# Dilated attention of a two-block network: projecting groups 1 and 2 from contiguous token tiles instead of strided ones

## The chip, the cores and the metric

The kernel runs on one core of one Trainium2 chip. The metric is device time in microseconds, from the start of the program to its end; the number given is the median of three runs.

## What is computed

Two transformer blocks over 512 latent tokens of width 1024 run one after the other. The change lies in the first mixer of the second block, a dilated attention with 15 heads of 64, in three groups of five heads. Group 0 attends to near neighbours; group 1 attends within the tokens of equal remainder modulo 4, group 2 within those of equal remainder modulo 16. What the reference does, cut to that mixer:

```python
DIL_PAIRS = ((128, 1), (512, 4), (2048, 16))

def _by_stride(t, dil):
    B, G, S, dh = t.shape
    return t.reshape(B, G, S // dil, dil, dh).transpose(0, 1, 3, 2, 4).reshape(B * G * dil, S // dil, dh)

def dilated_window_mixer(h, w_qkv, w_o, cos, sin):
    qkv = (h @ w_qkv).reshape(B, S, 3, A_HEADS, HEAD_DIM_2).transpose(2, 0, 3, 1, 4)
    q = apply_rope_2(qkv[0], cos, sin)
    k = apply_rope_2(qkv[1], cos, sin)
    v = qkv[2]
    for g, (window, dil) in enumerate(DIL_PAIRS):
        sl = slice(g * G, (g + 1) * G)
        half = window // (2 * dil)
        o, lse = banded_attention(_by_stride(q[:, sl], dil), _by_stride(k[:, sl], dil),
                                  _by_stride(v[:, sl], dil), half)
        ...
    alpha = jax.nn.softmax(jnp.stack(lses, axis=0), axis=0)
    o = jnp.concatenate([outs[g] * alpha[g][..., None] for g in range(3)], axis=1)
    return o.transpose(0, 2, 1, 3).reshape(B, S, A_HEADS * HEAD_DIM_2) @ w_o
```

## The kernel before

Activations lie feature-major in SBUF: chunk c of `X` is 128 features by 512 tokens, kept as two float32r parts, high and low, whose sum is the float32 value (class `Feat`). A product needs three matmuls per chunk, high by high, high by low and low by high (`mm`, L153 to L155). A weight unit is loaded by SyncE's queue into a `raw` buffer, of which there are three, cast by ScalarE (L135) and completed by a subtraction on VectorE (L136) into one of six `w` buffers.

`tm_gemm` (L234) makes token-major products: for each tile of 128 tokens, 8 chunks by 3 matmuls, the stationary operand being 128 tokens of `X` and the moving one 320 columns of weights here. A tile's second step, `late`, comes after the next tile's matmuls.

`mixer_a` (L1178) calls `project(g)` (L1196) for groups 1, 2, 0. Each project makes q, k and v: three products of four token tiles. A q or k tile is evicted from PSUM with a scale (L1205), rotated by four VectorE operations (L1173 to L1176), turned by three TensorE transposes (L1211) and copied into place (L1212). A v tile is copied out of PSUM into `V` (L1219). `scores` (L1223) multiplies q and k of a tile and adds the mask (L1246, L1248), takes the maximum (L1253) and the exponential (L1255). `values` (L1259) turns the probabilities (L1266) and multiplies them with `V` (L1274). Groups 1 and 2 write their output rows to DRAM (L1278), and group 0 reads them back (L1229) and merges all three.

In groups 1 and 2 the tokens of one tile are those of equal remainder modulo 4. `toks` (L1191) makes that order where the tile enters the product, by a view of `X` that takes every fourth token:

```python
return lambda a: a.rearrange("p (i r) -> p r i", r=4)[:, t, :]
```

So q, k and v come out in the order that the attention needs, and the rotation table `k_rope_a` holds one order for each group.

The program's order is set in three ways. `project(1)` is emitted alone, then `project(2)` in turns with `attention(1)`, then `project(0)` in turns with `attention(2)`, and `attention(0)` with filler from the next layer's `ple_proj`. A list scheduler that works from a timeline of its own then fixes the order on every engine. Buffers of a tag go round: three PSUM buffers `mm`, four SBUF buffers `t2`.

Of the kernel before, what the change touches and what calls it, by code (L numbers as in the profile page):

```python
# [10 lines left out]
F32 = mybir.dt.float32  # L11
# [6 lines left out]
P = 128  # L18
# [3 lines left out]
LAT = 512  # L22
# [18 lines left out]
class Feat:  # L41
    """Feature-major activations as two float32r parts: chunk c is [128 features, T tokens]."""
# [34 lines left out]
class Net:  # L77
# [54 lines left out]
    # ---------------------------------------------------------------- basics  # L132
    def split(self, hi, lo, src, eng=None):
        """hi + lo = src with two float32r parts; src in PSUM or SBUF."""
        self.nc.scalar.copy(hi, src)  # L135
        (eng or self.nc.vector).tensor_sub(lo, src, hi.bitcast(F32))  # L136
# [13 lines left out]
    def mm(self, out, l, r, first, last):  # L150
        """out += l.T @ r with l, r = (hi, lo) pairs."""
        mm = self.nc.tensor.matmul
        mm(out, lhsT=l[0], rhs=r[0], start=first, stop=False)  # L153
        mm(out, lhsT=l[0], rhs=r[1], start=False, stop=False)  # L154
        return mm(out, lhsT=l[1], rhs=r[0], start=False, stop=last)  # L155

    def mm_late(self, out, pairs, first, last):
        """The sum over (l, r) pairs of mm, the products with the low parts of r at the end."""
# [4 lines left out]
    def bias_rows(self, rows, mul=1.0):  # L163
        """Up to three rows of 512 as pairs of float32r parts: row q on partitions 32 q, 32 q + 1, zeros below."""
# [18 lines left out]
    def fm_gemm(self, X, W, cols, cb, lead=0):  # L183
        """Feature-major products: for each tuple of 128-wide column starts, out[128 cols, T] each -> cb(i, *ps).
        The first `lead` tuples run in two halves of the tokens, the first halves first."""
# [48 lines left out]
    def tm_gemm(self, X, W, c0, n, cb, br=None, k0=0, nk=None, kw0=None, toks=None, steps=False,  # L234
                slack=1, feats=None):
        """Token-major products: out[128 tokens, n cols] for each token tile -> cb(t, ps)."""
# [25 lines left out]
    def tm_pair(self, X, W, cb, kw0):  # L262
        """Token-major products with both 512-wide column halves of W, all of a token tile's in a row -> cb(t, n, ps)."""
# [31 lines left out]
    def fill_behind(self, n):  # L295
        """Filler that may not start before the tensor engine's last marked instruction."""
        with self.tc.issue_after(self.pe_mark.ins):
            self.fill(n)
# [4 lines left out]
    def transpose_in(self, src, X, t):  # L303
        """src [128 tokens, 128*nch] float32 -> token tile t of X."""
# [18 lines left out]
    def moments(self, out, halves):  # L323
        """Mean and variance of the row made of the two 512-wide pieces -> out [128, 2]."""
# [5 lines left out]
    # ---------------------------------------------------------------- per-layer vectors as columns  # L330
# [45 lines left out]
    # ---------------------------------------------------------------- ada  # L376
# [21 lines left out]
    def ada_first(self, S, x):  # L398
        """Shift and scale of the first layer's mixer, both streams: the context's on all partitions (returned as
        1 + scale, shift), the other's rows to DRAM."""  # L400
# [39 lines left out]
    def ada_out(self, l, n, o, src, nrow):  # L440
        """Modulation rows n (512 wide) of nrow streams: (src + bias), scaled for its kind -> DRAM."""
# [5 lines left out]
    def ada(self, l, n0, n1):  # L447
        """Both streams' modulation rows on the tensor engine."""
# [23 lines left out]
    def ada_vec(self, l, n0, n1):  # L472
        """The same with the sums over a partition's rows on the vector engine; the context has two rows only."""
# [38 lines left out]
    # ---------------------------------------------------------------- layer norms and modulation  # L512
    def mod_rows(self, l, s, i):
        """(1 + scale, shift) rows of modulation i (0: mixer, 1: ffn)."""
# [13 lines left out]
    def first_h(self, S, x, l, bc=None, then=None, xs=None):  # L528
        """Modulated input h of the first layer: X (Feat)."""
# [24 lines left out]
    def ln_prep(self, g, b, mod, gate):  # L554
        """Broadcast rows for a layer norm: gate, g, b and (if modulated) A, B."""
# [21 lines left out]
    def ln_finish(self, S, y, t, st_in, bc, xout, h_out, done=None):  # L577
        """y [128, 1024] token-major -> x (to DRAM xout, or kept in rms_x) and modulated h via h_out(t, h)."""
# [33 lines left out]
    # ---------------------------------------------------------------- first block: attention  # L612
    def head_norm(self, ps, nh, gain, rope_t):
        """RMS norm of nh heads of 128, gain, rotary -> SBUF tile [128, nh*128]."""
# [29 lines left out]
    def heads_T(self, src, nh, dst):  # L644
        """src [128 tok, nh*128] -> transposed heads, split into dst(hl) [128, nh, 128]."""
# [17 lines left out]
    def kv(self, l, kT, tiles):  # L663
        """For each (X, t, o, V, rotate): token tile t of X, keys (heads normed, rotated) into kT[kv][128, hl, o : o + 128],
        values into V[128, hl, tile, 256]."""
# [25 lines left out]
    def attend(self, nt, q, kT, vs, nkeys, o_dram, sums, gap):  # L691
        """One kv head: q(t) [128 d, hl, 4 heads, 128]; unnormalised O^T of heads h, h + 1 to o_dram(t, h)
        [128 d, 2, 128], the rows' sums to sums(t, h) [128, 1]."""
# [3 lines left out]
        def turned(Ps, k0):  # L697
            """Key chunks k0, k0 + 1 of two heads' probabilities, transposed."""
# [53 lines left out]
    def inverse_rows(self, sums, nt):  # L752
        """sums [128 tokens, nt, 8 heads] -> 1 / sums as rows [8 heads, tokens] in DRAM."""
# [11 lines left out]
    # ---------------------------------------------------------------- first block: merge of the branches  # L765
    def conv_gemm(self, l, S, X, convh, chains, chains2):
        """Gated input of the depthwise convolution; its taps go to `chains` (vector engine) and
        `chains2` (products on the scalar engine, sums on GpSimd)."""
# [75 lines left out]
    def pool_branch(self, l, S, X, m, between):  # L844
        """Pooling branch with its gate, added to m; `between` supplies other work."""
# [67 lines left out]
    def conv_ln(self, l, S, convh, C):  # L913
        """Layer norm and silu of the convolution, split into C."""
# [45 lines left out]
    def chunked(self, T, tag="s8"):  # L960
        """8 feature-major float32 chunks [128, T]."""
# [23 lines left out]
    def out_ln(self, S, M, W, bias, bc, xin, xout, h_out):  # L985
        """y = ALPHA x + gate (M @ W + bias); layer norm."""
# [19 lines left out]
    # ---------------------------------------------------------------- first block: ffn  # L1006
# [74 lines left out]
    # ---------------------------------------------------------------- second block  # L1081
    def rms_norm(self, xt, g):
        """x / rms(x) * g, in a new tile."""
# [10 lines left out]
    def add_out(self, X, W, x, done, k0=0, nk=None, kw0=None):  # L1094
        """x += X.T @ W, token tile by token tile; done(t, x(t)) after the second half."""
# [27 lines left out]
    def ple_proj(self, i, tag="w"):  # L1123
        """p @ w_ple_proj, halved, to DRAM."""
# [38 lines left out]
    def rope_small(self, v, r, cos, sin):  # L1163
        """In place rotation of the first 2r entries of the last dim of v [128, h, d]; cos, sin [128, 2r]."""
# [13 lines left out]
    def mixer_a(self, x, X, done):  # L1178
        nc, A = self.nc, self.A
        W = A["a_w_qkv_2"][0]  # L1180
        rp = self.sb([P, 3, 4, 32], F32, "rpa")
        nc.sync.dma_start(rp, A["k_rope_a"].rearrange("g (t p) d -> p g t d", p=P))
# [4 lines left out]
        # rows of groups 1, 2: unnormalised output, negative maxima, sums  # L1187
# [3 lines left out]
        def toks(g, t):  # L1191
            if g == 0:
                return lambda a: a[:, t * P : t * P + P]
            return lambda a: a.rearrange("p (i r) -> p r i", r=4)[:, t, :]

        def project(g):  # L1196
            tk = [toks(g, t) for t in range(4)]
            T = []
            for which in range(2):
                dst = self.sb([P, 3, 512], F32, "s8")  # L1200

                def cb(t, ps, which=which, dst=dst):
# [3 lines left out]
                    self.rope_small(q[:, 0:320].rearrange("p (h d) -> p h d", d=64), 8, rp[:, g, t, 0:16], rp[:, g, t, 16:32])  # L1206

                    def late():
# [3 lines left out]
                        nc.scalar.copy(dst[:, :, t * P : t * P + P], tp)  # L1212
# [3 lines left out]
                yield from self.tm_gemm(X, W, 960 * which + 320 * g, 320, cb, toks=tk, steps=True)  # L1216
                T.append(dst)
            V = self.sb([P, 4, 320], F32, "s8")
            yield from self.tm_gemm(X, W, 1920 + 320 * g, 320, lambda t, ps: nc.scalar.copy(V[:, t, :], ps) and None,  # L1219
# [324 lines left out]
def first_block(net, stop=None):  # L1544
# [18 lines left out]
    def mix(l, S, X, kT, vs, nkeys, rope, bc_mod, xin, xout, h_out, before_out=None, extra=None):  # L1563
# [30 lines left out]
        n = 0  # L1594
# [252 lines left out]
```

## Time and profile before

| | us |
|---|---|
| three runs | 4112.67, 4114.3, 4116.21 |
| median | 4114.3 |
| span of the profiled execution, first to last instruction | 4108.2 |
| median less span (launch and end; the profiled execution has no other time of its own listed) | 6.1 |
| TensorE busy in the span | 3835.9 (93%) |
| VectorE, ScalarE, GpSimd busy | 2729.5, 1537.3, 1055.7 |

TensorE is shown as two rows: PE, the matmuls, and PEld, the loads of stationary operands, which overlap the matmuls. The duration of a matmul overlaps its neighbours', so a stretch is best read by the distance from start to start. The granted clock (PEclk) is a share of 2.4 GHz: 1.00 is that level, 0.50 is 1.2 GHz.

### The profile page before, as it was taken

The numbers are of one execution on the slowest core, as the hardware profiler recorded it, in microseconds if no ns is written. First come the engines' busy times: TensorE is split into PE (matmuls) and PEld (weight loads), VectorE is DVE, ScalarE is ACT, GpSimd is POOL, SyncE is SP. The second block draws the span as 40 slices with busy tenths as digits, with TensorE's granted clock in tenths as the row PEclk, the third lists the DMA queues.
The fourth block names the chain that finished last, engine by engine and source line by source line (L and its number), as shares of the span: only waits on it lengthen the run. The fifth ranks groups of instructions, "written<-read, shape, count | busy, mean of one in ns | idle before, by whom it ended". The sixth has DMA issues, their size and how long they took to land.

```text
span 4108.2 us, 49603 instructions
## 1 busy us (share of the span) xinstructions
PE 3835.9 (93%) x18765; PEld 3179.4 (77%) x18765; DVE 2729.5 (66%) x3713; ACT 1537.3 (37%) x2685; POOL 1055.7 (26%) x1028
## 2 busy tenths in 40 slices
PE   7788999699898999999989999999999999999999
PEld 4678787477777887777767788889778888778887
DVE  4998799966989666789986645551354336764444
ACT  3535444234343332344324233332433224653333
POOL 3554422574544001422364200010000001420000
PEclk9789999899999999999999999999999999999999
DMA  6456322454566455321333423331223332123332
GB/s 204 118 141 212 94 62 85 116 151 153 179 217 190 154 162 166 112 67 54 99 96 115 128 86 116 119 98 45 88 86 99 96 96 78 24 67 108 98 98 92
DMA packets 544825, 469.04 MB, mean 114 GB/s; under 512 B 31734, under 2 KB 435806, under 8 KB 544586
## 3 DMA queue, kind: packets, MB, share of 16 engines
q1 hardware_dynamic: 544506, 465.61, 37.5%
q8 instruction: 147, 2.41, 0.2%
q14 instruction: 92, 0.75, 0.1%
q0 software_dynamic: 80, 0.26, 0.0%
HBM read 442.32 MB, written 23.49 MB: 113 GB/s over the span
## 4 chain that ended last, share of the span: by engine, by line
PE 61%; DVE 25%; DMA 4%; issue 4%; ACT 3%; POOL 2%; SPq 0%; POOLq 0%; ACTq 0%; DVEq 0%
PE mm L153 18%; PE mm L154 18%; PE mm L155 18%; DVE s L787 10%; DVE w L136 4%; DVE s L136 2%; DVE s L504 1%; DVE st L740 1%; DMA w<-in_w_ada 1%; DMA raw<-in_w_in 1%; ACT w L135 1%; PE acc L161 1%; PE b L1246 1%; PE b L310 1%; ACT s L135 1%
## 5 line engine op out<-in xcount | busy, mean ns | idle before, releaser
L153 PE MATMUL mm<-s,w 128*128 128x512 f32 (+1 forms) x3072 | 1125.8, 369 | 79.8 <-ACT pad L1019 20.5
L154 PE MATMUL mm<-s,w 128*128 128x512 f32 (+1 forms) x3072 | 1119.3, 365 | 10.6 <-DVE s L136 10.6
L155 PE MATMUL mm<-s,w 128*128 128x512 f32 (+1 forms) x3072 | 1117.8, 365 | 2.2 <-DVE w L136 2.2
L135 ACT CAST w<-raw 128x1024 fp32r<-128x1024 f32 (+4 forms) x673 | 689.5, 1030 | 843.1 <-PE mm L155 427.2
L136 DVE TENSOR_TENSOR w<-raw,w 128x1024 fp32r<-128x1024 f32 (+3 forms) x517 | 670.3, 1300 | 309.5 <-ACT w L135 304.5
L153 PE MATMUL mm<-w,s 128*128 128x512 f32 (+2 forms) x1960 | 766.5, 392 | 10.9 <-ACT s L135 5.3
L154 PE MATMUL mm<-w,s 128*128 128x512 f32 (+2 forms) x1960 | 756.8, 387 | 1.3 <-DVE w L136 1.3
L155 PE MATMUL mm<-w,s 128*128 128x512 f32 (+2 forms) x1960 | 753.8, 387 | 1.3 <-DVE s L136 1.3
L153 PEld LDWEIGHTS mm<-s,w 128*128 128x128 f32 x3072 | 599.3, 196 | 192.9 <-ACT pad L1019 22.7
L154 PEld LDWEIGHTS mm<-s,w 128*128 128x128 f32 x3072 | 601.5, 196 | 95.6 <-DVE s L136 12.5
L155 PEld LDWEIGHTS mm<-s,w 128*128 128x128 f32 x3072 | 600.5, 196 | 89.3 <-DVE w L136 2.6
L787 DVE SCALAR_TENSOR_TENSOR s<-pad,cols,s 128x512 f32<-128x512 f32 (+1 forms) x690 | 573.2, 873 | 1.1
L136 POOL TENSOR_TENSOR w<-raw,w 128x1024 fp32r<-128x1024 f32 (+1 forms) x156 | 418.5, 2685 | 475.9 <-ACT w L135 475.6
L153 PEld LDWEIGHTS mm<-w,s 128*128 128x128 f32 x1960 | 396.4, 202 | 91.3 <-issue 14.5
L155 PEld LDWEIGHTS mm<-w,s 128*128 128x128 f32 x1960 | 396.0, 202 | 67.1 <-DVE s L136 2.6
L154 PEld LDWEIGHTS mm<-w,s 128*128 128x128 f32 x1960 | 396.9, 203 | 64.0 <-DVE w L136 2.7
L320 POOL TENSOR_SCALAR st<-st 128x1 f32<-128x1 f32 (+2 forms) x91 | 33.3, 366 | 1215.4 <-ACT s L1086 902.1
L1101 DVE TENSOR_TENSOR s<-s,mm 128x512 f32<-128x512 f32 x80 | 54.7, 686 | 171.7 <-PE mm L155 171.7
L136 DVE TENSOR_TENSOR s<-b,s 128x256 fp32r<-128x256 f32 (+2 forms) x224 | 119.6, 546 | 51.1 <-ACT s L135 50.2
L135 ACT CAST s<-b 128x256 fp32r<-128x256 f32 (+2 forms) x224 | 104.2, 475 | 126.0 <-DVE s L136 76.0
L1117 DVE TENSOR_TENSOR t<-t 128x512 f32<-128x512 f32 x64 | 44.3, 693 | 153.4 <-ACT t L1116 153.4
L1017 POOL MEMSET pad<- 128x1 f32 x66 | 7.5, 116 | 469.6 <-DVE t L1024 463.0
(271 smaller groups left out, 4407.8 us busy)
## 6 DMA issues: line engine op xcount, KB each, us to landing
raw<-in_w_up SPq DMA_DIRECT2D x196, 512.0 KB
raw<-in_w_in SPq DMA_DIRECT2D x180, 512.0 KB
raw<-in_w_down SPq DMA_DIRECT2D x130, 512.0 KB
w<-in_w_ada SPq DMA_DIRECT2D x48, 512.0 KB
raw<-in_w_ada SPq DMA_DIRECT2D x32, 512.0 KB
s<-d SPq DMA_DIRECT2D x26, 512.0 KB
raw<-in_conv_pw_w SPq DMA_DIRECT2D x24, 512.0 KB
raw<-in_w_out SPq DMA_DIRECT2D x24, 512.0 KB
```

The lines of the kernel that those rows point to most:

```text
L135: self.nc.scalar.copy(hi, src)
L136: (eng or self.nc.vector).tensor_sub(lo, src, hi.bitcast(F32))
L153: mm(out, lhsT=l[0], rhs=r[0], start=first, stop=False)
L154: mm(out, lhsT=l[0], rhs=r[1], start=False, stop=False)
L155: return mm(out, lhsT=l[1], rhs=r[0], start=False, stop=last)
L161: self.nc.tensor.matmul(out, lhsT=l, rhs=r, start=first and n == 0, stop=last and n == len(terms) - 1)
L310: self.pe_mark = nc.tensor.transpose(ps[:, c, :], src[:, (c0 + c) * P : (c0 + c + 1) * P], self.ident)
L504: nc.vector.scalar_tensor_tensor(out=v, in0=w, scalar=c, in1=v, op0=ALU.mult, op1=ALU.add)
L740: self.mark = nc.vector.reduce_max(out=s[:, 0:1], in_=S[:, :nkeys], axis=AX.X, negate=True)
L787: nc.vector.scalar_tensor_tensor(out=o, in0=pad[:, k : k + T], scalar=self.col("dww", 8 * k + j), in1=o, op0=ALU.mult, op1=ALU.add)
L1101: nc.vector.tensor_add(x(t)[:, cs], x(t)[:, cs], ps)
L1117: nc.vector.tensor_mul(r, r, r)
```

## The change

Groups 1 and 2 are now projected like group 0, from tiles of 128 tokens that follow each other, with one rotation table. The order modulo 4 is made afterwards. For q and k it is made by the copy of the turned tile: it reads every fourth column of the PSUM tile and writes four runs of 32 columns. For v, whose tokens lie on partitions, it is made by a trip through DRAM: each tile is copied to a `t2` buffer and written to `vd`, and when all four are there one load brings them back with partition i holding rows 4 i to 4 i + 3.

```diff
-        rp = self.sb([P, 3, 4, 32], F32, "rpa")
-        nc.sync.dma_start(rp, A["k_rope_a"].rearrange("g (t p) d -> p g t d", p=P))
+        rp = self.sb([P, 4, 32], F32, "rpa")
+        nc.sync.dma_start(rp, A["k_rope_a"].rearrange("(t p) d -> p t d", p=P))
...
-        def toks(g, t):
-            if g == 0:
-                return lambda a: a[:, t * P : t * P + P]
-            return lambda a: a.rearrange("p (i r) -> p r i", r=4)[:, t, :]
-
         def project(g):
-            tk = [toks(g, t) for t in range(4)]
...
-                        nc.scalar.copy(dst[:, :, t * P : t * P + P], tp)
+                        if g == 0:
+                            nc.scalar.copy(dst[:, :, t * P : t * P + P], tp)
+                        else:
+                            nc.scalar.copy(dst.rearrange("p j (r i) -> p j r i", r=4)[:, :, :, 32 * t : 32 * t + 32],
+                                           tp.rearrange("p j (i r) -> p j r i", r=4))
...
-                yield from self.tm_gemm(X, W, 960 * which + 320 * g, 320, cb, toks=tk, steps=True)
+                yield from self.tm_gemm(X, W, 960 * which + 320 * g, 320, cb, steps=True)
...
-            yield from self.tm_gemm(X, W, 1920 + 320 * g, 320, lambda t, ps: nc.scalar.copy(V[:, t, :], ps) and None,
-                                    toks=tk, steps=True)
+            vd = self.dram([LAT, 320]) if g else None
+
+            def cb(t, ps):
+                if g == 0:
+                    nc.scalar.copy(V[:, t, :], ps)
+                    return
+                v = self.sb([P, 512], F32, "t2")[:, :320]
+                nc.scalar.copy(v, ps)
+                nc.sync.dma_start(vd[t * P : t * P + P, :], v)
+
+            yield from self.tm_gemm(X, W, 1920 + 320 * g, 320, cb, steps=True)
+            if g:
+                nc.sync.dma_start(V, vd.rearrange("(i r) d -> i r d", r=4))
...
-    out["k_rope_a"] = np.stack([rot(8, t.reshape(-1, d).T.reshape(-1)) for d in (1, 4, 4)])
+    out["k_rope_a"] = rot(8, t)
```

The change also moves instructions, since a tile of the product now needs only one token tile of `X`, and a tile of the attention needs all four turned tiles of q and k.

TensorE, where `project(1)` begins, before. `mm_21265` is the last product of the filler, L310 turns the last token tile into `X`, `mm_21319` and `mm_21353` are the q tiles 0 and 1.

```order
L155 MATMUL mm_21265<-s_3073_20869,s_3063_20838 128x512
L310 MATMUL b_3140_21275<-ident_66,s_3121_21172 128x128 x8
L153 MATMUL mm_21319<-w_21306,s_3103_21032 128x320
L154 MATMUL mm_21319<-w_21306,s_3103_21032 128x320
L153 MATMUL mm_21353<-w_21306,s_3103_21032 128x320
L154 MATMUL mm_21353<-w_21306,s_3103_21032 128x320
```

The same place in the changed kernel. The first ten matmuls of q tile 0 stand directly behind `mm_21265`; the rows begin with the eleventh:

```order
L154 MATMUL mm_21319<-w_21311,s_3104_21035 128x320
L155 MATMUL mm_21319<-w_21311,s_3104_21035 128x320
L153 MATMUL mm_21319<-w_21311,s_3105_21038 128x320
L310 MATMUL b_3140_21275<-ident_66,s_3121_21172 128x128 x8
L154 MATMUL mm_21319<-w_21311,s_3105_21038 128x320
L155 MATMUL mm_21319<-w_21311,s_3105_21038 128x320
L153 MATMUL mm_21319<-w_21311,s_3105_21038 128x320
```

Thirteen matmuls of q tile 0 have come ahead of the last transposes into `X`.

TensorE, the end of the k product of group 1, before. `t_3185` to `t_3195` are rotated k tiles, `b_3228` the first scores of group 1, `mm_21603` the last k tile's product.

```order
L155 MATMUL mm_21603<-w_21488,s_3106_21041 128x320
L1246 MATMUL b_3228_21858<-s_3172_21475,s_3145_21303 128x128
L1211 MATMUL mm_21628<-ident_66,t_3190_21594 128x128 x3
L1248 LDWEIGHTS identb_71
L1248 MATMUL b_3228_21858<-msk_21298,identb_71 128x128
L1246 MATMUL b_3228_21858<-s_3172_21475,s_3145_21303 128x128
```

The same place in the changed kernel, up to the first matmuls of v:

```order
L153 MATMUL mm_21603<-w_21488,s_3106_21041 128x320
L154 MATMUL mm_21603<-w_21488,s_3106_21041 128x320
L155 MATMUL mm_21603<-w_21488,s_3106_21041 128x320
L1206 MATMUL mm_21628<-ident_66,t_3190_21594 128x128 x3
L1206 MATMUL mm_21642<-ident_66,t_3195_21633 128x128 x3
L153 MATMUL mm_21664<-w_21651,s_3103_21032 128x320
L154 MATMUL mm_21664<-w_21651,s_3103_21032 128x320
L155 MATMUL mm_21664<-w_21651,s_3103_21032 128x320
```

The scores have left this place, so the last k tile's transposes stand directly behind the transposes of the tile before it, as they already did at the end of q.

SyncE's queue in the changed kernel, around the trip of v of group 1. `d_21648` is the DRAM buffer, `s_3199` is `V`, the `raw` loads ahead are the last of group 2's k, those between are of group 2's v, those behind of group 0's q.

```order
L141 DMA raw_22000<-in_a_w_qkv 128x2x320
L1226 DMA d_21648<-t_3208_21689 128x320
L1226 DMA d_21648<-t_3210_21717 128x320
L1226 DMA d_21648<-t_3212_21745 128x320
L141 DMA raw_22215<-in_a_w_qkv 128x3x320
L1226 DMA d_21648<-t_3214_21773 128x320
L141 DMA raw_22220<-in_a_w_qkv 128x3x320
L141 DMA raw_22225<-in_a_w_qkv 128x2x320
L1230 DMA s_3199_21647<-d_21648 128x1280
L141 DMA raw_22396<-in_a_w_qkv 128x3x320
```

Before, only the `raw` loads stood here; the four writes and the load of `V` are new, and so are their waits.

## Rows read from the trace of the kernel before

**Rows 1.** Engines over the span, from the page: busy us, share, instructions.
```profile
PE 3835.9 (93%) x18765; PEld 3179.4 (77%) x18765; DVE 2729.5 (66%) x3713; ACT 1537.3 (37%) x2685; POOL 1055.7 (26%) x1028
```

**Rows 2.** Busy time by stretch: groups 1 and 2, then group 0's projection.
```profile
core 0: us, PE busy (x) PEld busy (x) DVE busy (x) ACT busy (x) POOL busy (x), PEclk, DMA share, GB/s
2717.00:2880.00 163.00, 160.24 (x746) 155.40 (x747) 37.11 (x99) 42.59 (x105) 2.83 (x19) 0.98 0.17 49
2880.00:2942.00 62.00, 62.00 (x424) 57.44 (x424) 15.88 (x48) 19.57 (x66) 0.91 (x6) 1.00 0.20 60
```

**Rows 3.** Longest wait of PE from 2717 to 2942: total, times, longest us.
```profile
PE mm L1211 <- DVE t L1176: 2.5, 2, 2.0
```

**Rows 4.** Instructions by line and shape, 2717 to 2945: count, busy, mean ns.
```profile
L153 PE MATMUL mm<-w,s 128*128 128x320 f32 x288 | 108.3, 376 | 0.5 <-ACT s L135 0.5
```

**Rows 5.** Timeline, group 1, strided: first and last of 18 matmuls, a load.
```profile
2731.10 0.40 PE L153 MATMUL mm<-w,s 128*128 128x320 f32 x1
...
2735.07 0.40 PE L155 MATMUL mm<-w,s 128*128 128x320 f32 x1
...
2731.17 0.33 PEld L154 LDWEIGHTS mm<-w,s 128*128 128x128 f32 x1
```

**Rows 6.** Timeline, group 0, contiguous: first and last of 25 matmuls, a load.
```profile
2902.01 0.31 PE L153 MATMUL mm<-w,s 128*128 128x320 f32 x1
...
2905.53 0.31 PE L153 MATMUL mm<-w,s 128*128 128x320 f32 x1
...
2902.01 0.19 PEld L154 LDWEIGHTS mm<-w,s 128*128 128x128 f32 x1
```

**Rows 7.** Timeline of PE where group 1 begins; idle before in brackets.
```profile
2715.76 1.07 PE L310 MATMUL b<-ident,s 128*128 128x128 f32 x8 [0.53 <-DVE s L1088]
2717.29 0.54 PE L153 MATMUL mm<-w,s 128*128 128x320 f32 x1 [0.46 <-ACT s L135]
```

**Rows 8.** Timeline of PE and VectorE at the end of group 1's q.
```profile
2741.27 0.49 PE L1211 MATMUL mm<-ident,t 128*128 128x128 f32 x3
2743.72 0.52 PE L1211 MATMUL mm<-ident,t 128*128 128x128 f32 x3 [1.96 <-DVE t L1176]
...
2741.09 1.16 DVE L136 TENSOR_TENSOR w<-raw,w 128x960 fp32r<-128x960 f32 x1 [0.94 <-ACT w L135]
...
2742.60 0.83 DVE L136 TENSOR_TENSOR w<-raw,w 128x640 fp32r<-128x640 f32 x1
2743.34 0.23 DVE L1176 TENSOR_TENSOR t<-rp,rp 128x80 f32<-128x80 f32 x1
```

**Rows 9.** Timeline of PE at half clock after that wait, strided.
```profile
2746.32 0.47 PE L153 MATMUL mm<-w,s 128*128 128x320 f32 x1
...
2748.72 0.47 PE L153 MATMUL mm<-w,s 128*128 128x320 f32 x1
```

**Rows 10.** Busy time by stretch around the two falls of the granted clock.
```profile
2744.00:2748.00 4.00, 4.00 (x19) 4.00 (x17) 0.00 (x0) 0.48 (x1) 0.15 (x1) 0.73 0.55 192
2748.00:2752.00 4.00, 4.00 (x19) 4.00 (x17) 0.70 (x4) 0.44 (x1) 0.00 (x0) 0.84 0.00 0
...
2772.00:2776.00 4.00, 4.00 (x19) 3.29 (x19) 1.02 (x3) 2.81 (x14) 0.15 (x1) 0.65 0.37 122
```

**Rows 11.** Chain, contiguous 512-column matmuls at half clock, by start.
```profile
2955.00 0.43 PE mm L153
2955.43 0.43 PE mm L154
```

**Rows 12.** Line 1212, copies of turned tiles: ns min, median, max.
```profile
L1212 ACT COPY s<-mm x24: 473/480/512, 2729.9 to 2927.4; 128x384 f32<-128x384 f32 x24
```

**Rows 13.** Timeline, group 2's rows written, read back and first used.
```profile
2945.49 0.38 SPq L1278 DMA_DIRECT2D d<-row  x1
2949.20 2.56 SPq L1229 DMA_DIRECT2D s<-d  x4
2954.77 0.16 DVE L1286 TENSOR_TENSOR st<-s 128x5 f32<-128x5 f32 x1
```

More of the change, by code (lines that the diff above doesn't have):

```diff
@@ L1205, in cb @@
                     nc.scalar.activation(q[:, 0:320], ps, AF.Copy, scale=0.125 if which == 0 else 1.0)
-                    self.rope_small(q[:, 0:320].rearrange("p (h d) -> p h d", d=64), 8, rp[:, g, t, 0:16], rp[:, g, t, 16:32])
+                    self.rope_small(q[:, 0:320].rearrange("p (h d) -> p h d", d=64), 8, rp[:, t, 0:16], rp[:, t, 16:32])
                     def late():
```

## The prediction

> **What bounds the kernel now.** I began with the busy shares of the page: TensorE is busy 93% of the span, the next engine 66% [rows 1]. So the question is what TensorE does in the stretch that the change touches, and the second view, busy time by stretch, gives that: groups 1 and 2 with the attention of group 1 take 163 us, of which PE is busy 160 and the loads of stationary operands (PEld) 155; group 0's projection with the attention of group 2 takes 62 us, PE busy throughout [rows 2]. PE's longest wait in all of this totals 2.5 us [rows 3]. No other engine is busy for more than a third of either [rows 2]. The stretch is as long as TensorE's own instructions, so a gain can only come from making those shorter.
>
> The third view is the timeline of TensorE, read by distance from start to start. In group 1, whose stationary tokens lie four elements apart, 18 matmuls start within 3.97 us, 17 steps of 0.2335 us; a load of the stationary operand takes 0.33 us [rows 5]. In group 0, with the same shape but contiguous tokens, 25 matmuls start within 3.52 us, 24 steps of 0.1467 us; the load takes 0.19 us [rows 6]. The moving operand is the same 320 columns in both, the granted clock is 0.98 and 1.00 [rows 2]. The load is what differs, and in groups 1 and 2 it sets the pace.
>
> **The change, part by part.**
>
> (a) *Contiguous stationary tokens.* The trace holds 288 matmuls of 128x320 on each of three lines [rows 4], 864 for three groups, so 576 in groups 1 and 2. Each goes from 0.2335 to 0.1467 us: 576 x 0.0868 = **-50.0 us**, all on the path, as TensorE hardly waits there [rows 3]. This leans on rows of the same program, engine, shape and clock.
>
> (b) *The start of group 1.* Before, TensorE idled 0.53 us ahead of the last transposes into X and 0.46 us ahead of the first product [rows 7], because every strided tile needs all four token tiles. Thirteen matmuls now stand ahead of those transposes, 13 x 0.1467 = 1.9 us of work: **-1.0 us**.
>
> (c) *The ends of q and k.* At the end of q in group 1 two sets of transposes stand back to back, and the second waited 1.96 us for the rotation of the last tile; VectorE was held up by the subtractions of the next weights, 1.16 and 0.83 us, which stand ahead of the rotation's last step [rows 8]. That chain starts when the 18th of the tile's 24 matmuls lets go of the second weight unit. From there TensorE has six matmuls left, which cover 1.4 us now and 0.88 us then: the wait grows by 0.5 to 2.5 us. At the end of k the scores of group 1 lay between the two sets and hid the same chain. The scores need all four turned tiles now and have moved behind v, so the wait appears there too, at 2.5 us. Together **+3.0 us**. In group 2 other attention work stands between, as in group 0, which did not wait [rows 2].
>
> (d) *The granted clock.* After the wait at q the clock fell: 0.73 and 0.84 in two stretches of 4 us, so (0.27 + 0.16) x 4 x 2 = 3.4 us at 1.2 GHz; a second fall of some 2.8 us came among the scores [rows 10]. At that level strided matmuls stepped by 2.40 us / 9 = 0.267 us [rows 9], hardly slower than at 2.4 GHz. Contiguous ones lose more: 512 columns step by 0.43 us there [rows 11], which I scale to an estimated 0.269 us for 320. I allow one spell of 3.4 us behind each of the two waits: 13 matmuls x (0.269 - 0.147) = 1.6 us, twice 3.2 us. The old spells cost 0.4 + 0.3 us, which (a) left out. Net **+2.5 us**; were there no falls, it would be -0.7.
>
> (e) *Reading every fourth column.* The 16 copies of turned q and k tiles in groups 1 and 2 took 0.48 us each [rows 12]. The trace has no such copy with a step. From below I take the 0.48 us (a step gives no reason for a gain), from above twice that. Even 16 x 0.48 = 7.7 us more would lie on an engine with 43 us of work in 163 [rows 2]: the turned tiles are wanted a tile or more later, and the three PSUM buffers go round once in a tile and a half. I count 0, and keep 7.7 us for the range.
>
> (f) *The trip of v.* Eight copies go to another buffer, at no new cost; eight writes of 160 KB and two loads of 640 KB are new, 2.6 MB. The nearest row is the trip of group 2's output: written at 2945.49, read back by a load issued at 2949.20, first used at 2954.77, so 3.7 us to the second step and 9.3 us in all [rows 13]. Two weight loads stand between the last write and the load of V. They wait for buffers that are freed by about two casts and subtractions of 1.16 us each [rows 8], so I add 4 us: 13 us. Between the end of v's product and the first product with V the new order has 124 matmuls, 18.2 us, and two sets of scores. The cover holds, and I count 0; without it the bound is 2 x 9.3 = 18.6 us. Behind the waiting V load on SyncE's queue stand group 0's q weights, not wanted before group 2's v is done; GpSimd's clearing of the next t2 buffer would wait for a write four tiles back, 14 us against 3.7 us. One rotation table for three, and the smaller load, cost nothing that anything waits for.
>
> Sum: -50.0 - 1.0 + 3.0 + 2.5 = **-45.5 us**. The span was 4108.2 and would be 4062.7. The median of the runs stands 6.1 us above the span, outside the change: 4114.3 - 45.5 = **4068.8 us**. A cross-check: the old 163 us hold 576 x 0.2335 = 134.5 us of strided products, so 28 us of everything else, which the change only reorders.
>
> **The rivals.**
>
> *Stalls at every turn.* Matmuls that are faster by a third leave ScalarE and VectorE less cover for the next weights, and the wait of (c) with its fall of the clock could come at all six ends of q, k and v. Four more at 2.5 + 1.6 us are 16.4 us: 4085.2 us. For it: the same order of subtractions and rotation at each end [rows 8]. Against it: group 0 ran at exactly the new pace, with the same weights to prepare and an attention between, and TensorE was busy for 62.00 of 62 us [rows 2].
>
> *The trip of v shows.* If the weight loads ahead of V's load are late, TensorE stands before the first product with V. At 10 us for each group, that is 4088.8 us. Against it the 5 us and more of slack in (f).
>
> *The loads do not get shorter.* Then the distance in rows 5 would be due to something other than the step. The gain of (a) falls away and only the start (-1.0), the new wait at k (+2.0) and a small fall (+0.4) are left: 4115.7 us. For it: nothing in the rows. The Trainium skill, TensorE: Matmul & The Clock Gate, section LDWEIGHTS, says that the load's time goes by its columns alone; as all loads here have 128 columns, by that rule (a) would be nothing and the time would be this one. The trace disagrees: 0.33 against 0.19 us for the same 128 columns [rows 5, 6].
>
> *The clock stays down.* If the reordered first part, with two waits in 30 us, kept TensorE at 1.2 GHz through both groups, contiguous matmuls would step by 0.269 us against the old 0.2335: 576 x 0.0355 = +20.4 us, with (b) and (c) 4136.7 us, slower than before. It decides where more than (0.2335 - 0.1467) / (0.269 - 0.1467) = 71% of the matmuls run at the lower level. For it: the clock did fall after a 2 us wait [rows 8, 10]. Against it: it came back within 3.4 us, and stood at 1.00 through the whole of group 0 [rows 2].
>
> **How the numbers follow.** The forecast has 0.78, stalls at every turn 0.12, the trip 0.04, no shorter loads 0.04, the clock 0.02. A measurement of this kernel can tell 0.2%, 8.2 us, from no change. The first three cases are faster by more: 0.94. The fourth lies within: 0.04; the last is slower: 0.02. The range starts where (c) and (d) cost nothing, 4114.3 - 51.7 = 4062.6, less 2.6 us because the scheduler also shuffles the end of the block ahead; it ends at 4088, which holds the forecast with (e) on the path (4076.5) and the first rival (4085.2).
>
> **What would show it.** Right: in the changed profile the 128x320 matmuls of groups 1 and 2 step by 0.147 us and their loads take 0.19 us; the stretch from the first product to group 0's takes some 117 us in place of 163; two waits of PE for the last step of the rotation, near 2.5 us each; no wait of PE for V. Wrong: a step that stays above 0.2 us (the third rival), waits of PE for weights or rotation at more than two ends (the first), a wait of L1284 for a DMA (the second), a granted clock well below 1.00 through the stretch (the last).

## The result and the profile after

The changed kernel takes 4067.14 us (median of 4 runs, 4057.85 to 4070.36) against 4113.49 us (4 runs, 4109.56 to 4116.21) for the kernel before on the same chip: ratio 0.9883, 95% interval 0.9869 to 0.9897. It is faster by 46.4 us. The forecast was 4068.8 us, 45.5 us faster, with a range of 4060 to 4088.

Engines over the span, from the page of the changed kernel, beside [rows 1]:

```profile
PE 3785.9 (93%) x18765; PEld 3128.9 (77%) x18765; DVE 2729.4 (67%) x3713; ACT 1535.6 (38%) x2685; POOL 1059.9 (26%) x1028
```

PE's busy time went from 3835.9 to 3785.9 us with the same 18765 matmuls: 50.0 us less. That this is the size of term (a) to a tenth is luck: a second trace of the changed kernel has 3790.5 us, and the stretches below are the better reading. VectorE has the same work to 0.1 us.

Busy time by stretch, from the first 128x320 matmul of group 1 to the first of group 0, and from there to group 0's last (columns as in [rows 2]):

```profile
2709.88:2824.68 114.80, 109.96 (x743) 104.78 (x743) 37.17 (x100) 42.33 (x107) 2.98 (x20) 0.99 0.28 87
2824.68:2889.23 64.55, 64.55 (x434) 59.99 (x433) 17.16 (x50) 20.89 (x69) 1.06 (x7) 0.97 0.23 74
```

The kernel before, between the same two matmuls of groups 1 and 2:

```profile
2717.29:2878.68 161.39, 158.92 (x735) 154.07 (x735) 36.06 (x98) 41.30 (x102) 2.77 (x19) 0.98 0.16 47
```

From there to group 0's last it took 63.01 us, by the starts of its matmuls. So groups 1 and 2 became 46.6 us shorter and group 0 1.5 us longer. PE idled 114.80 - 109.96 = 4.84 us in the first stretch. What PE waited for, from 2690 to 2960 us (total us, times, longest):

```profile
PE mm L1206 <- DVE t L1176: 4.8, 2, 2.4
PE b L310 <- DVE w L136: 3.3, 1, 3.3
PE b L310 <- DVE s L136: 3.0, 1, 3.0
PE b L1276 <- ACT s L1265: 1.2, 1, 1.2
```

L1206 is L1211 of before [rows 3]: the two waits are the ends of q and of k in group 1, and they are the 4.84 us of idle time. The other three waits lie outside the two stretches. No wait is on L1284, the product with V.

Timeline of TensorE in the changed kernel (start, us, engine, instruction, idle time before it): the first product of group 1, beside [rows 7], then the end of its q, beside [rows 8] and, for the matmuls behind, [rows 5]:

```profile
2709.88 0.42 PE L153 MATMUL mm<-w,s 128*128 128x320 f32 x1 [0.42 <-ACT t L1142]
...
2725.60 0.49 PE L1206 MATMUL mm<-ident,t 128*128 128x128 f32 x3
2728.51 0.52 PE L1206 MATMUL mm<-ident,t 128*128 128x128 f32 x3 [2.42 <-DVE t L1176]
2728.78 0.39 PE L153 MATMUL mm<-w,s 128*128 128x320 f32 x1
2729.01 0.31 PE L154 MATMUL mm<-w,s 128*128 128x320 f32 x1
2729.16 0.31 PE L155 MATMUL mm<-w,s 128*128 128x320 f32 x1
2729.30 0.31 PE L153 MATMUL mm<-w,s 128*128 128x320 f32 x1
...
2729.89 0.19 PEld L155 LDWEIGHTS mm<-w,s 128*128 128x128 f32 x1
```

The matmuls start 0.147 us apart, where before it was 0.2335, and a load takes 0.19 us in place of 0.33. VectorE at the same place:

```profile
2725.94 1.16 DVE L136 TENSOR_TENSOR w<-raw,w 128x960 fp32r<-128x960 f32 x1 [0.16 <-ACT w L135]
...
2727.39 0.82 DVE L136 TENSOR_TENSOR w<-raw,w 128x640 fp32r<-128x640 f32 x1
2728.13 0.23 DVE L1176 TENSOR_TENSOR t<-rp,rp 128x80 f32<-128x80 f32 x1
```

The rotation's last step starts behind two subtractions, as in [rows 8], and TensorE starts 0.15 us after it ends. At the end of k the same rows come again, with 2.42 us of idle time.

### The profile page after: what moved, and what is told of

The parts are those of the page before. It is cut to its first block, busy times and chain, and to the rows that moved or that the text cites. A ratio compares the mean times of both kernels' runs of the same rounds, so it can differ in the third digit from the quotient of the medians.

```text
span 4056.1 us, 49639 instructions
## 1 busy us (share of the span) xinstructions
PE 3785.9 (93%) x18765; PEld 3128.9 (77%) x18765; DVE 2729.4 (67%) x3713; ACT 1535.6 (38%) x2685; POOL 1059.9 (26%) x1028
## 4 chain that ended last, share of the span: by engine, by line
PE 60%; DVE 26%; DMA 5%; issue 4%; ACT 3%; POOL 2%; SPq 0%; ACTq 0%; POOLq 0%; DVEq 0%
PE mm L153 18%; PE mm L154 18%; PE mm L155 18%; DVE s L787 10%; DVE w L136 4%; DVE s L136 2%; DVE s L504 1%; DVE st L740 1%; DMA w<-in_w_ada 1%; ACT w L135 1%; DMA raw<-in_w_in 1%; PE acc L161 1%; PE b L1256 1%; PE b L310 1%; DVE t L1024 1%
## 5 line engine op out<-in xcount | busy, mean ns | idle before, releaser
L153 PE MATMUL mm<-w,s 128*128 128x512 f32 (+2 forms) x1960 | 750.4, 384 | 11.9 <-ACT s L135 5.6
L153 PEld LDWEIGHTS mm<-s,w 128*128 128x128 f32 x3072 | 599.8, 196 | 188.0 <-ACT pad L1019 21.2
L154 PE MATMUL mm<-w,s 128*128 128x512 f32 (+2 forms) x1960 | 741.6, 379 | 1.3 <-DVE w L136 1.3
L155 PE MATMUL mm<-w,s 128*128 128x512 f32 (+2 forms) x1960 | 739.0, 379 | 1.3 <-DVE s L136 1.3
L153 PEld LDWEIGHTS mm<-w,s 128*128 128x128 f32 x1960 | 370.3, 189 | 92.3 <-issue 14.2
L155 PEld LDWEIGHTS mm<-w,s 128*128 128x128 f32 x1960 | 370.1, 189 | 67.6 <-DVE s L136 2.6
L154 PEld LDWEIGHTS mm<-w,s 128*128 128x128 f32 x1960 | 370.5, 189 | 63.6 <-DVE w L136 2.7
L504 DVE SCALAR_TENSOR_TENSOR s<-w,cond,s 128x512 f32<-128x512 f32 x112 | 101.0, 921 | 43.4 <-DMA w<-in_w_ada 43.0
```

The source lines that it names most:

```text
L504: nc.vector.scalar_tensor_tensor(out=v, in0=w, scalar=c, in1=v, op0=ALU.mult, op1=ALU.add)
```

## The experiments

All times below are medians of timed runs. They were taken on three chips, each with its own runs of the kernel before: the changed kernel again, the step of four, the doubled trip and the transposes put off on the first; the step of two, the run without the trip and the run with v strided on the second; the step of three on the third. From one chip to another the ratios and the stretches compare better than the medians. The stretches are read from the starts of matmuls in each run's trace, between the same matmuls as above.

### The changed kernel again

No edit.

> The changed kernel once more, beside the runs that follow, to have its time and its stretches on the same chip. All theories expect the same as its first runs: 4058 to 4070 us, a ratio to the kernel before near 0.988, 2.4 us of wait at the ends of q and of k in group 1, and 128x320 matmuls that step by 0.147 us.

Measured: 4067.05 us, ratio 0.9872 [0.9857, 0.9886], against 4119.22 us for the kernel before on this chip. Groups 1 and 2 took 114.70 us, group 0 64.55. The gain reads 46.4 us in one comparison and 52.2 in the other, while the changed kernel's median and its stretches agree to 0.1 us. It is the kernel before that has another median, 4119.22 in place of 4113.49 us; no trace shows where those 5.7 us lie. Single executions of the changed kernel spread as far, and between its two traces, 4057.85 and 4063.54 us, the difference lies ahead of the change: the first 128x320 matmul started at 2709.88 in the first and at 2715.72 in this one.

### The stationary operand alone, back to a step of four

```diff
-                yield from self.tm_gemm(X, W, 960 * which + 320 * g, 320, cb, steps=True)
+                yield from self.tm_gemm(X, W, 960 * which + 320 * g, 320, cb, toks=tk, steps=True)
...
-            yield from self.tm_gemm(X, W, 1920 + 320 * g, 320, cb, steps=True)
+            yield from self.tm_gemm(X, W, 1920 + 320 * g, 320, cb, toks=tk, steps=True)
```

`tk` is the view of before, every fourth token, for groups 1 and 2; everything else is the changed kernel.

> The changed kernel with one thing put back: the products of groups 1 and 2 again take every fourth token as the stationary operand, while the stepped evictions, the trip of v, the one rotation table and the later scores stay (so the order of q, k and v is made twice and the attention of groups 1 and 2 works on other tokens). Theory of the load: the 576 matmuls step by 0.233 us again, their loads take 0.33 us, the stretch of groups 1 and 2 grows by some 47 us from 115 and the time comes to about 4116 us, ratio to before 1.000 to 1.002, slightly above it by the new wait at the end of k. Theory of the order (the gain came from moving the scores and starting group 1 earlier): most of the gain stays, about 4070 to 4080 us.

Measured: 4119.28 us, ratio 1.0003 [0.9993, 1.0012]. Busy time of groups 1 and 2, and two rows of the timeline, ten steps apart:

```profile
2724.23:2889.34 165.11, 160.58 (x734) 155.56 (x735) 36.07 (x98) 41.13 (x102) 2.72 (x18) 0.96 0.19 57
```

```profile
2726.47 0.39 PE L153 MATMUL mm<-w,s 128*128 128x320 f32 x1
...
2728.81 0.39 PE L155 MATMUL mm<-w,s 128*128 128x320 f32 x1
...
2726.31 0.33 PEld L153 LDWEIGHTS mm<-w,s 128*128 128x128 f32 x1
```

2.34 us for ten steps: 0.234 us each, with loads of 0.33 us. The whole gain is gone with the step, 52.2 us of it beside the changed kernel in the same comparison, and the stretch is longer by 50.4 us. So the gain is in the loads. The step of the copies, the trip of v and the later scores, all still there, bring nothing by themselves: beside the kernel before the stretch is 3.7 us longer, 2.0 of it by more waits for the rotation (4.5 us in three, against 2.5). Only the start of group 1 went back with the step: as every tile needs all four token tiles again, the transposes into X stand ahead of the first product, with 0.39 and 0.46 us of idle time. That part is term (b), 1 us at most.

### The stationary operand with a step of two

```diff
+            tk = [lambda a, t=t: a[:, 256 * (t // 2) : 256 * (t // 2) + 256].rearrange("p (i r) -> p r i", r=2)[:, t % 2, :] for t in range(4)] if g else None
```

passed as `toks` in the same two lines.

> Changed kernel, but the stationary tokens of groups 1 and 2 lie two elements apart (every second token) in place of side by side; the rows of q, k and v then come in another order, so that part of the output differs. Theory 1, the load of the stationary operand goes with the stretch of memory that it reads: step 2 lies halfway, load about 0.26 us, 128x320 matmuls 0.19 us apart, groups 1 and 2 some 25 us longer than in the changed kernel, time about 4092 us, ratio to before 0.994. Theory 2, the load is slowed only from a step of four on (by the Trainium skill, SBUF - State Buffer, 16-byte cachelines need two hits per line, which a step of two 4-byte elements gives): load 0.19 us, 0.147 us apart, time as the changed kernel, 4067 us, ratio 0.988. Rival: any step at all costs the full price, 0.33 us and 0.2335 us apart: about 4117 us, ratio 1.000.

Measured: 4069.13 us, ratio 0.9882 [0.9866, 0.9899]. Timeline, group 1:

```profile
2717.34 0.31 PE L155 MATMUL mm<-w,s 128*128 128x320 f32 x1
...
2722.17 0.31 PE L155 MATMUL mm<-w,s 128*128 128x320 f32 x1
...
2717.34 0.20 PEld L153 LDWEIGHTS mm<-w,s 128*128 128x128 f32 x1
```

From the first row to the second are 33 steps in 4.83 us, 0.146 us each; a load takes 0.20 us. A step of two costs nothing that TensorE's pace shows, as theory 2 has it; its other half, that the price begins at a step of four, is tried next. Groups 1 and 2 took 116.38 us, 1.7 more than the 114.70 of the changed kernel run again. About 1.1 us of that is the clock: it fell behind both waits here, where in the changed kernel it fell behind the second alone, and nine more products ran 0.267 us apart. The rule of the Trainium skill, SBUF — State Buffer, section Specifications (TRN2), that a 16-byte line must be hit twice for full bandwidth, agrees with 0.20 us at a step of two and 0.33 us at a step of four.

### The stationary operand with a step of three

```diff
+            tk = [lambda a, t=t: a[:, 32 * t : 32 * t + 384].rearrange("p (i r) -> p r i", r=3)[:, 0, :] for t in range(4)] if g else None
```

> As the run with the step of two, but the stationary tokens of groups 1 and 2 lie three elements apart (the rows of q, k and v are other tokens' then, so that part of the output differs). Steps of one and two gave 0.147 us from matmul to matmul, a step of four 0.2335 us. Theory 1, the load's time goes with the number of 16-byte lines that it touches (64 for a step of two, 96 for three, 128 for four), and shows once it passes the matmul: 0.2335 x 96 / 128 = 0.175 us from start to start, 576 x 0.028 = 16 us above the changed kernel, about 4083 us, ratio 0.992. Theory 2, any step that leaves fewer than two elements to a 16-byte line costs the full price: 0.2335 us, about 4117 us, ratio 1.000. Rival 3, only a step of a whole line costs something: 0.147 us, 4067 us, ratio 0.988.

Measured: 4076.58 us, ratio 0.9913 [0.9895, 0.9931]. Timeline, group 1:

```profile
2721.13 0.34 PE L155 MATMUL mm<-w,s 128*128 128x320 f32 x1
...
2724.77 0.34 PE L155 MATMUL mm<-w,s 128*128 128x320 f32 x1
...
2724.10 0.26 PEld L155 LDWEIGHTS mm<-w,s 128*128 128x128 f32 x1
```

21 steps in 3.64 us: 0.1733 us, where theory 1 said 0.175 and theories 2 and 3 said 0.2335 and 0.147. Groups 1 and 2 took 133.17 us, 18.5 more than in the changed kernel run again, where 16 was worked out; the wait at q's end came at 2.25 us and a further one of 0.74 us appeared at an earlier turn. These tokens need more than one token tile too, so another 1.2 us of idle time came round the last transposes into X. The median is 9.5 us above that of the changed kernel on another chip, less than the stretch says, while the ratios, 0.9913 and 0.9872, differ by some 17 us; in this trace the stretch began at 2708.34 us, 7.4 us earlier than in the changed kernel's second trace. So the pace settles the question here, not the median: from a step of two on, the load's time rises evenly with the step, by some 0.065 us for each element. Theory 2 of the run before fell too in what it said of a step of three. Whether the cause is the count of 16-byte lines of theory 1 or the stretch of memory read, these steps can't tell, since both are in proportion to the step.

### Only q and k from contiguous tokens

The changed kernel with v again from every fourth token and straight into `V`, so without the trip; `tk` is that of the step of four:

```diff
...
-                v = self.sb([P, 512], F32, "t2")[:, :320]
-                nc.scalar.copy(v, ps)
-                nc.sync.dma_start(vd[t * P : t * P + P, :], v)
...
-            yield from self.tm_gemm(X, W, 1920 + 320 * g, 320, cb, steps=True)
-            if g:
-                nc.sync.dma_start(V, vd.rearrange("(i r) d -> i r d", r=4))
+                nc.scalar.copy(V[:, t, :], ps)
+
+            yield from self.tm_gemm(X, W, 1920 + 320 * g, 320, cb, toks=tk, steps=True)
```

> Half of the change: q and k from contiguous tokens with the order made at the eviction, v again from every fourth token of X and straight into V without a trip. Load theory: 384 of 576 matmuls keep the gain, 192 fall back by 0.0868 us each: 16.7 us above the changed kernel, about 4084 us, ratio 0.992; the v products step by 0.2335 us, those of q and k by 0.147 us. Rival (the trip costs something that this version saves): less than 14 us above the changed kernel. Rival (the gain sits in something other than the loads, such as the order of the work): no clear proportion to the count of strided matmuls.

Measured: 4084.05 us, ratio 0.9921 [0.9906, 0.9935], 17.0 us above the changed kernel (4067.05 on another chip) and 17.2 above the run without the trip on this one (4066.81, below). Groups 1 and 2 took 130.45 us, 15.75 more than the 114.70 of the changed kernel run again, where 16.7 was worked out. Timeline in the k of group 1 and in its v:

```profile
2737.72 0.31 PE L155 MATMUL mm<-w,s 128*128 128x320 f32 x1
2737.87 0.31 PE L153 MATMUL mm<-w,s 128*128 128x320 f32 x1
...
2755.88 0.39 PE L155 MATMUL mm<-w,s 128*128 128x320 f32 x1
2756.11 0.40 PE L153 MATMUL mm<-w,s 128*128 128x320 f32 x1
2756.34 0.40 PE L154 MATMUL mm<-w,s 128*128 128x320 f32 x1
```

The loss is proportional within about 1 us: a third of the matmuls strided again gives back about a third of the 50.0 us. So the gain of v's part of the change is there too, and the trip that pays for it doesn't take it away.

### The trip of v left out, and made twice

Left out: the four tiles are copied straight into `V`, the writes and the load are gone.

```diff
...
-                v = self.sb([P, 512], F32, "t2")[:, :320]
-                nc.scalar.copy(v, ps)
-                nc.sync.dma_start(vd[t * P : t * P + P, :], v)
+                nc.scalar.copy(V[:, t, :], ps)
...
-            if g:
-                nc.sync.dma_start(V, vd.rearrange("(i r) d -> i r d", r=4))
```

> Changed kernel, without the DRAM trip of v: the tiles are copied straight into V, whose rows then stay in token order, so the order modulo 4 of v is left out of the computation. Theory (the trip is covered): same time as the changed kernel within 3 us, 4064 to 4070 us, ratio 0.987 to 0.989; groups 1 and 2 take 114.7 us. Rival (part of the trip is on the path): 5 to 18 us faster, 4049 to 4062 us.

Measured: 4066.81 us, ratio 0.9876 [0.9862, 0.9891], groups 1 and 2 114.82 us (the changed kernel 114.80 and 114.70). Group 0, in which the trip of group 2's v ends, took 63.01 us in place of 64.55: the clock doesn't fall there (more on this in the last section).

Made twice: `V` is written to a second DRAM buffer and read again.

```diff
                 nc.sync.dma_start(V, vd.rearrange("(i r) d -> i r d", r=4))
+                vd2 = self.dram([LAT, 320])
+                nc.sync.dma_start(vd2.rearrange("(i r) d -> i r d", r=4), V)
+                nc.sync.dma_start(V, vd2.rearrange("(i r) d -> i r d", r=4))
```

> The changed kernel with the trip of v doubled: V is written to a second DRAM buffer and read again. Theory that the trip is covered: the load of V of group 1 goes out 21 us before the first product with V, so 6 to 9 us more are hidden there; in group 2 the cover is shorter, some 15 us, and still holds: 0 to 2 us more than the changed kernel. Rival (the trip or SyncE's queue behind it is on the path): 12 to 18 us more, with TensorE waiting before the products with V or for weights of the next product.

Measured: 4065.32 us, ratio 0.9871 [0.9855, 0.9888], groups 1 and 2 114.70 us. SyncE's queue in this kernel, group 1 (start of the issue), and the first product with V:

```profile
2765.92 0.34 SPq L1226 DMA_DIRECT2D d<-t  x1
2766.67 1.12 SPq L141 DMA_DIRECT2D raw<-in_a_w_qkv  x2
2769.90 0.34 SPq L1230 DMA_DIRECT2D s<-d  x1
2775.26 0.34 SPq L1232 DMA_DIRECT2D d<-s  x1
2778.24 0.32 SPq L1233 DMA_DIRECT2D s<-d  x1
...
2791.01 1.22 PE L1287 MATMUL acc<-s,s 128*128 128x64 f32 x10
```

Each step waits for the landing of the one before, so the rows give the trip's price: 3.98 us from the last write to the load (the two weight loads fit between), 5.36 us from the load to what needs `V`, 9.3 us in all. The second trip is another 2.98 us and the same load. By that, all of it is over some 7 us ahead of the first product with V at 2791.01. Neither leaving the trip out nor doubling it moves the stretch of groups 1 and 2 by more than 0.12 us, and doubling it leaves group 0 at 64.55 us: TensorE never waits for it.

### The last tile's transposes behind the next product

If TensorE only lacks other work while VectorE ends the rotation, the waits at the ends of q and k go when it turns the last tile one token tile later:

```diff
...
             late.append(cb(t, ps))
+            if owed and t == 0:
+                self.call(owed.pop())
             if steps:
                 yield
+        if keep:
+            owed.append(late.pop())
```

`project` passes `owed`, with `keep=True` for q and k, in every group.

> The changed kernel with the transposes of the last q tile put behind the first product of k, and those of the last k tile behind the first product of v, in every group. Theory of the wait (the last rotation stands behind the subtractions of the next weights and nothing covers it): the two waits of 2.42 us go, and with them the fall of the clock behind the second (13 matmuls of 0.267 in place of 0.147 us, 1.6 us): about 6.4 us less than the changed kernel, near 4060 us if that stands at 4067, and a stretch of groups 1 and 2 of some 108 us in place of 115. Rival (another wait takes its place: a later tile waits for weights, a buffer or the copies): no change within 2 us.

Measured: 4056.42 us, ratio 0.9848 [0.9833, 0.9862], 10.6 us below the changed kernel in the same comparison. Groups 1 and 2, then group 0:

```profile
2711.17:2819.09 107.92, 107.92 (x742) 103.23 (x743) 37.20 (x100) 42.31 (x107) 2.98 (x20) 1.00 0.30 93
2819.09:2882.21 63.12, 63.12 (x433) 58.44 (x432) 17.09 (x50) 20.98 (x69) 1.06 (x7) 1.00 0.24 76
```

PE is busy for all of the 107.92 us, at a granted clock of 1.00. Against 114.70 that is 6.8 us less: 4.84 us of waits, about 1.5 us of half clock behind the second, and 0.4 us not placed. Group 0 is 1.4 us shorter, as the clock doesn't fall there. The remaining 2.4 us of the difference are of the size of the spread of the stretch's start, and aren't a result of the edit that these runs could show. This is the fastest version of the study.

## Why the prediction was right

The forecast's case came: a gain made by the loads, reduced a little by two waits and the clock. Term by term, with the step that measured each:

- **(a) Contiguous stationary tokens, -50.0 us.** PE's busy time in the stretch fell from 158.92 to 109.96 us; without the falls of the clock, which cost 0.7 us of the first and 1.5 of the second, that is 49.8. The step of four put back lengthened the stretch by 50.4, (b) and (c) included. The pace of 0.1467 us, taken from group 0 [rows 6], held in groups 1 and 2. The third rival, that the loads do not get shorter, fell: by the rule of the Trainium skill, TensorE: Matmul & The Clock Gate, section LDWEIGHTS, columns alone would set the load's time, and 128 columns took 0.19, 0.20, 0.26 and 0.33 us at steps of one, two, three and four.
- **(b) The start of group 1, -1.0 us.** Of the two idle times of [rows 7] the 0.53 us ahead of the transposes is gone; the other shrank from 0.46 to 0.42 us, since the first product waits for ScalarE (L1142), not for the transposes. So -0.6 us. It can't be seen in the medians: in the traces of the changed kernel and its variants, that with the step of four left out, the stretch began anywhere from 2708.34 to 2721.14 us.
- **(c) The ends of q and k, +3.0 us.** Two waits of 2.42 us, 4.84 in all, in place of 2.5 [rows 3], 1.96 of it at q's end: +2.3. What the prediction left out is that the other 0.5 us, a wait at the first turn of group 1's q, would go. The chain named in the prediction is what the rows show, and putting the transposes off removed both.
- **(d) The clock, +2.5 us.** The number held and its place didn't. A fall was allowed behind each of the two waits. In the first trace there was none behind q's; one came behind k's, and one in group 0, which had run at 1.00 throughout [rows 2]:

```profile
2745.50:2749.50 4.00, 2.99 (x16) 3.02 (x17) 0.86 (x2) 0.48 (x1) 0.00 (x0) 0.76 0.92 297
2749.50:2753.50 4.00, 4.00 (x24) 4.00 (x24) 0.00 (x0) 0.43 (x1) 0.00 (x0) 0.81 0.04 16
...
2832.00:2836.00 4.00, 4.00 (x25) 2.83 (x24) 0.70 (x4) 0.92 (x2) 0.15 (x1) 1.00 0.26 104
2836.00:2840.00 4.00, 4.00 (x19) 4.00 (x19) 0.89 (x2) 1.85 (x10) 0.00 (x0) 0.57 0.00 0
```

  Each cost about 1.5 us: from 2747.45 to 2751.04 there are 14 steps, 3.59 us where 14 x 0.1467 = 2.05. At 1.2 GHz matmuls stepped by 0.267 us, where 0.269 had been scaled from 512 columns [rows 11]. With the old spells of 0.7 us gone this is +2.3. The estimate of a fall's size was sound; that the total held is luck, as one of the two falls foreseen did not come and one that was not foreseen did. The number of falls is not steady either: the run with a step of two had one behind each wait and another in group 0, the run without the trip a single one, behind k's.
- **(e) Every fourth column, 0.** The copies (line L1210 now) took 474 / 478 / 514 ns, against 473 / 480 / 512 [rows 12]. The upper bound of twice the price was far off; the lower one was the truth.
- **(f) The trip of v, 0.** Estimated at 13 us, it takes 9.3, as the row it was taken from says [rows 13]; the 4 us added for the weight loads weren't needed, as the writes took as long to land. The first product with V came at 2788.35, 21.2 us after the load's issue at 2767.12 and 26.0 after v's last product (2762.33), so the cover was longer than the 18.2 us of matmuls worked out, to which the prediction gave no time for the two sets of scores.

Sum by these: -50.0 - 0.6 + 2.3 + 2.3 = -46.0 us, against -45.5 forecast. That the medians' 46.4 us lies so near as well is luck: its interval runs from 42 to 54 us, and the second comparison gave 52.2. The traces give the same stretch as a whole: from the end of the last work ahead of group 1's first instruction, idle time included, to group 0's first product it was 163.45 us (2715.23 to 2878.68) and is 115.22 (2709.46 to 2824.68), so -48.2, and group 0's +1.5 makes -46.7; 0.7 us of that has no term. The expected "117 us in place of 163" is 114.80 in place of 161.39, counted from the first product.

One step was wrong without harm: the 6.1 us between span and median were put down to launch and end. The profiled execution of the changed kernel took 4057.85 us for a span of 4056.1, 1.75 us more, so most of the 6.1 us was a profiled execution of before that was faster than the median. As the change was subtracted from the median, the forecast didn't suffer.

The first rival (stalls at every turn) didn't come: two waits, both at ends of group 1. The second (the trip shows) fell by the two runs on the trip, the fourth (the clock stays down) by the granted clock of 0.99 in the stretch.

What stays open: why the stretch begins up to 13 us earlier or later from trace to trace, so whether a gain or a loss of a few us ahead of the change is hidden in there; why the kernel before read 4113.49 us in one comparison and 4119.22 in the other (gains of 46.4 and 52.2 us); and what made the clock fall in group 0.

## What to carry to other kernels

Where TensorE's load of the stationary operand is as busy as its matmuls, measure the distance from start to start for each form of the operand: a step of four float32 elements raised it by 59% at 320 moving columns, and the reorder was free where it was put into a PSUM eviction or a DRAM trip with 20 us of cover. When matmuls get faster, look for the chain on another engine that they used to hide, here the rotation behind the next weights' subtractions, and give TensorE other work there: that brought 6.8 us more in the stretch. Compare stretches between the same matmuls of two traces, since executions of the same kernel here differ by several us for reasons ahead of the change.

## What the runs showed of the hardware

The price of a strided stationary operand is not all or nothing. With float32r tokens and 128 columns, start to start at 2.4 GHz and load:

| step, elements | start to start, us | load, us |
|---|---|---|
| 1 | 0.147 | 0.19 |
| 2 | 0.146 | 0.20 |
| 3 | 0.173 | 0.26 |
| 4 | 0.2335 | 0.33 |

At the lower clock it is not seen at all: contiguous matmuls (behind k's end in the changed kernel, under (d)) and those with steps of four [rows 9] both step by 0.267 us. Reading PSUM with a step of four float32 in ScalarE's copy cost nothing (478 against 480 ns). And the granted clock fell to 1.2 GHz (0.57 as the mean of a row) behind 4 us in which PE was busy throughout, among the short matmuls of the scores (the last two rows of the windows under (d)). The run without the trip at the same place of the program:

```profile
2843.00:2847.00 4.00, 4.00 (x25) 2.96 (x24) 0.70 (x4) 0.92 (x2) 0.15 (x1) 1.00 0.00 2
2847.00:2851.00 4.00, 4.00 (x28) 3.87 (x29) 0.89 (x2) 1.85 (x10) 0.00 (x0) 1.00 0.00 0
```

It stayed at 1.00 there. The run with a step of two, which has the trip, had such a fall in its group 0 too, but later, among the scores ahead of v:

```profile
2878.80:2882.80 4.00, 4.00 (x18) 4.00 (x17) 0.82 (x1) 1.87 (x10) 0.15 (x1) 0.50 0.23 75
```

Of the seven traces with the trip four had a fall in group 0: the changed kernel twice and the doubled trip at the same place of the program, the step of two at this one. The steps of three and four and the transposes put off had none, nor had the three traces without the trip, that of the kernel before among them. So the trip alone doesn't bring it; whether it has a part in it these traces don't settle. No idle time of TensorE stood ahead of it: in the first trace the last was the wait at k's end, which ended at 2746.51, 90 us before. What does bring it wasn't tried.
